# Scale and shift of the second norm: from the stored token rows to the transposed gathered tokens

## The chip, the cores and the metric

The kernel runs on one core of a Trainium2 chip. The core has five engines, each with an instruction queue of its own that runs in order: PE (TensorE, matmuls and transposes; its weight loads are listed as PEld), DVE (VectorE), ACT (ScalarE), POOL (GpSimd) and SP (SyncE, which here only issues DMAs). The engines wait for each other on semaphores. On-chip tiles lie in SBUF, matmul results in PSUM, the rest in DRAM. The metric is the device time of one execution in microseconds.

## What is computed

One layer of an encoder on 1024 tokens of 1024 channels in float32. A conditioning vector gives `shift1, scale1, gate1, shift2, scale2, gate2`. After the mixer has been added to `x`, the part that matters here is:

```python
h2 = rmsnorm(x, norm2_w) * (1.0 + scale2) + shift2          # per channel
aff = softmax(h2 @ w_router)                                # 16 experts
gates, idx = top_k(aff.transpose, 128)                      # each expert picks 128 tokens
xe = h2[idx]                                                # gather
y = (silu(xe @ w_gate) * (xe @ w_up)) @ w_down              # per expert, 1024 wide
x += gate2 * scatter_add(idx, y * gates)
```

`rmsnorm` divides a token's row by its root mean square `r` and multiplies by `norm2_w` per channel. So `h2` is `x` times a number per token, then a scale and a shift per channel.

## The kernel before

The framework in which the kernel is written takes the instructions in program order, with tiles from pools. A pool tag has a number of buffers, and a tile waits for a free one. A scheduling pass with durations of its own then fixes an order for each engine's queue. `issue_after(ins)` keeps instructions behind `ins` on the same engine.

**Projection stage** (`w_o`, L1278). Eight tiles of 128 tokens. For each tile, `wo_tile` (L1335) runs the output projection on PE; every factor is split into a high part, rounded to the matmul type, and the low rest, and three products (high-high, high-low, low-high) are summed. `wo_post` (L1352) follows for the tile before: it loads `x` (L1356, SP), adds the projection (L1359, DVE), transposes (PE, through the helper at L149), squares and sums the rows (L1368, ACT), gets `r` on DVE (`rsqrt1`, L125), computes the router's scores from the transposed rows with the scale already folded into `wr` (L1309) and the shift into `rc` (L1308), takes the softmax (L1376 to L1382; the exponential L1380 is ACT's) and transposes the scores. Then, in tiles 0 to 6, L1395 on DVE computes `x * r * g2`, where `g2` is the scale of all channels broadcast to 128 partitions; in the last tile this is L1398 on ACT and L1399 on POOL. L1400 on POOL adds the broadcast shift `sh2`, and L1401 (POOL's DMA queue) stores the row tile of `h2` to DRAM. `rsqrt1` returns -8 times the wanted factor, so the -0.125 in `g2` puts that right. `g2`, `sh2` and `norm2_w` come as broadcast DMAs on SP (L1290, L1291), and L1292 and L1293 combine them. The same vectors are also loaded as columns into `cols` (L1298 to L1303): columns 0 to 7 the shift, 8 to 15 the scale of the eight blocks of 128 channels.

Sorting the scores is DVE work too: `best_merge` after tile 3, `join_best` after tiles 5 and 7 and `threshold` at the end, made of `max`, `match_replace` and a merge network (`bitonic`, L1439 and L1440, min and max of 16x64 tiles; L1482 and L1484 on 16x128). From the threshold `choose` computes each token's slot in each expert.

**Expert stage** (`moe`, L1580), 16 experts one after the other. For expert `e`, `gather(e + 1)` is in program order first: a one-hot tile (L1543, DVE, in a buffer with the tag `y`, of which there are two), eight small matmuls (L1548), the list of rows (L1550 to L1552), and an indirect DMA on POOL's queue (L1605) that gathers 128 rows of `h2` into `xe`. The gathered rows are transposed in two halves of four blocks (`to_T`, L1592): four transposes into one PSUM tile (tag `dn`, two buffers), a cast to the high part on ACT (L1598) and a subtraction for the low part on DVE (L1599). The weights come by SP in pieces of 512 KB (24 per expert) into a ring of 31 SBUF tiles (`RING`, L39; one of its places is `hTl5`, where `sh2` lies before). Each piece is split on ACT (L1575) and DVE (L1576) into one of four pairs of tiles. PE multiplies tokens with the gate and up weights (L1629), ACT and DVE form `silu(gate) * up` (L1633, L1634, in a `y` buffer), which is transposed by `to_T` in turn, and PE multiplies with the down weights in eight blocks `k` (L1646). Within this last loop, at `k` of 5 and 6, the two halves of the next expert's tokens are transposed (L1640 to L1642). L1650 weights the result, and L1652, again on POOL's queue, adds it to the output rows in DRAM; it reads the same tile into which `xe` is gathered.

Of the kernel before, what the change touches and what calls it, by code (L numbers as in the profile page):

```python
# [7 lines left out]
F = mybir.dt.float32  # L8
# [4 lines left out]
AF = mybir.ActivationFunctionType  # L13
OP = mybir.AluOpType
# [4 lines left out]
D = 1024  # L19
S = 1024  # L20
NT = 8
C_Q, C_K, C_V, C_DQ, C_DK, C_DV, C_DZ, C_BA, C_G = 0, 512, 640, 768, 1280, 1792, 2304, 2816, 2848
EPS = 1e-6
NEXP = 16
# [61 lines left out]
class K:  # L86
# [1191 lines left out]
    def w_o(self):  # L1278
        nc, i, u, wk = self.nc, self.i, self.unit, self.ep
        self.mhl = [[u(g, (128, 8, 128), R, name="mhl") for g in gs] for gs in (("g1", "g2"), ("g14", "g15"))]  # L1280
        for ps, _ in self.wo_tile(0):
            pass
        g2, sh2 = (u(g, name="mod") for g in ("hTl4", "hTl5"))
        self.xs = [u(g, name="wx") for g in ("hTl6", "hTl7")]
        self.xTs = [u(g, (128, 8, 128), name="wxT") for g in ("hTh6", "hTh7")]
        self.ts = [u(g, name="wt") for g in ("g16", "g0", "wl")]
        self.gt2 = wk.tile([128, D], F, name="gt2")
        n2 = self.ts[2]
        for t, row in ((sh2, 1), (g2, 2), (self.gt2, 3)):
            nc.sync.dma_start(t, self.mod_d[row:row + 1].to_broadcast([128, D]))  # L1290
        nc.sync.dma_start(n2, i["norm2_w"].to_broadcast([128, D]))  # L1291
        nc.vector.scalar_tensor_tensor(g2, g2, 1.0, n2, op0=OP.add, op1=OP.mult)  # L1292
        nc.vector.tensor_scalar(g2, g2, -0.125, None, op0=OP.mult)  # L1293
        wr = wk.tile([128, 8, NEXP], F, name="wr", bufs=1)
        nc.sync.dma_start(wr, i["w_router"][0].rearrange("(k p) e -> p k e", p=128))
        rows = wk.tile([24, 128], F, name="rrows", bufs=1)
        for r, src in enumerate((self.mod_d[1:2], self.mod_d[2:3], i["norm2_w"])):
            nc.sync.dma_start(rows[r * 8:r * 8 + 8], src.rearrange("o (k p) -> (o k) p", p=128))  # L1298
        pc = self.pa.tile([128, 128], F, name="tr", bufs=2)
        self.transpose(pc[:, 0:24], rows)  # L1300
        cols = wk.tile([128, 24], F, name="rcols", bufs=1)
        nc.vector.tensor_copy(cols, pc[:, 0:24])
        nc.vector.scalar_tensor_tensor(cols[:, 8:16], cols[:, 8:16], 1.0, cols[:, 16:24], op0=OP.add, op1=OP.mult)  # L1303
        pr = self.pa.tile([128, NEXP], F, name="tr", bufs=2)
        for k in range(8):
            nc.tensor.matmul(pr, cols[:, k:k + 1].to_broadcast([128, 128]), wr[:, k], start=(k == 0), stop=(k == 7))
        rc = wk.tile([128, NEXP], F, name="rc", bufs=1)
        nc.vector.tensor_copy(rc, pr)  # L1308
        nc.vector.scalar_tensor_tensor(wr, wr, -0.125, cols[:, 8:16].unsqueeze(2).to_broadcast([128, 8, NEXP]),  # L1309
                                       op0=OP.mult, op1=OP.mult)  # L1310
        for j in range(NT):
            post = self.wo_post(j, ps, g2, sh2, wr, rc, wk)
            at = list(POSTS)
            for nxt, done in self.wo_tile(j + 1) if j + 1 < NT else ():
                while at and done > at[0]:
                    next(post, None)
                    at.pop(0)
            for _ in range(EARLY.get(j, 0)):
                self.ring_load()
            for _ in post:  # L1320
                pass
            ps = nxt
            if j == 3:
                rbest = wk.tile([NEXP, CAP], F, name="rbest", bufs=1)
                nc.scalar.copy(rbest, rev(self.best_merge(wk)))
            if j in JOINS:
                self.join_best(JOINS.index(j), rbest, wk)
        self.threshold(rbest, wk)
# [20 lines left out]
                                     start=(k == 0 and n == 0), stop=(k == 7 and n == 2))  # L1349
            yield pq, (s + 1) / len(steps)  # L1350

    def wo_post(self, j, pq, g2, sh2, wr, rc, wk):  # L1352
        nc, i = self.nc, self.i
        sl = slice(j * 128, (j + 1) * 128)
        x, t, xT = self.xs[j % 2], self.ts[j % 3], self.xTs[j % 2]
# [15 lines left out]
        r = self.rsqrt1(wk, ss, "r2")  # L1371
# [19 lines left out]
                nc.vector.tensor_copy(self.sc[p:p + NEXP, t0], pa[:NEXP, 64 * x2:64 * x2 + 64])  # L1391
        yield
        nc.gpsimd.dma_start(self.out[0, sl, :], x)
        if j < NT - 1:
            nc.vector.scalar_tensor_tensor(t, x, r, g2, op0=OP.mult, op1=OP.mult)  # L1395
        else:
            with self.tc.issue_after(ex):
                nc.scalar.activation(t, x, AF.Copy, scale=r)  # L1398
            nc.gpsimd.tensor_mul(t, t, g2)  # L1399
        nc.gpsimd.tensor_add(t, t, sh2)  # L1400
        nc.gpsimd.dma_start(self.h2_d[sl, :], t)  # L1401


# [176 lines left out]
    def moe(self):  # L1580
# [11 lines left out]
        def to_T(dst, src, q):  # L1592
# [5 lines left out]
            nc.scalar.copy(hi, pt)  # L1598
            nc.vector.tensor_sub(lo, pt, hi.bitcast(F))  # L1599

        def gather(e):
            nonlocal found
            with self.tc.issue_after(found) if e else ExitStack():
# [8 lines left out]
        gather(0)  # L1612
        first = found
        for q in range(2):
            to_T(xT, xe[:, q * 512:(q + 1) * 512], q)
        for e in range(NEXP):
            if e + 1 < NEXP:
                gather(e + 1)
# [18 lines left out]
            for k in range(8):  # L1637
                if k == 2:
                    to_T(aT, acts[1], 1)
                if e + 1 < NEXP and k in (5, 6):  # L1640
                    q = k - 5
                    to_T(xT, xe[:, q * 512:(q + 1) * 512], q)  # L1642
                w = weights()
                for n, (x, wi) in enumerate(passes(aT, w)):
                    for q in range(2):
# [41 lines left out]
```

## Time and profile before

| | us |
|---|---|
| median of 3 runs (lowest, highest) | 1728.37 (1728.33, 1729.34) |
| the profiled execution | 1728.42 |
| its span, first to last instruction | 1726.6 |
| PE, DVE, ACT, POOL busy | 1616.8, 1409.3, 907.1, 204.3 |

"Busy" is the time in which an engine had an instruction running, over the whole span. Matmuls are pipelined, and their ends are modelled, so a busy PE need not be PE at its best rate. In the lists in order of time, neighbouring instructions of one form are merged (x4 is four of them), and brackets tell how long the engine was idle before and what ended the wait.

### The profile page before, as it was taken

The numbers are of one execution on the slowest core, as the hardware profiler recorded it, in microseconds if no ns is written. First come the engines' busy times: TensorE is split into PE (matmuls) and PEld (weight loads), VectorE is DVE, ScalarE is ACT, GpSimd is POOL, SyncE is SP. The second block draws the span as 40 slices with busy tenths as digits, with TensorE's granted clock in tenths as the row PEclk, the third lists the DMA queues.
The fourth block names the chain that finished last, engine by engine and source line by source line (L and its number), as shares of the span: only waits on it lengthen the run. The fifth ranks groups of instructions, "written<-read, shape, count | busy, mean of one in ns | idle before, by whom it ended". The sixth has DMA issues, their size and how long they took to land. (4 is left out here: it accounts for less than half of the span.)

```text
span 1726.6 us, 30147 instructions
## 1 busy us (share of the span) xinstructions
PE 1616.8 (94%) x11131; PEld 1278.1 (74%) x11131; DVE 1409.3 (82%) x2470; ACT 907.1 (53%) x1352; POOL 204.3 (12%) x196
## 2 busy tenths in 40 slices
PE   6999999889999899699999999669999999999997
PEld 4777778677777677478887788557777777777786
DVE  6899897954667757789986567979999999999996
ACT  6654432122344213288871323347777777777775
POOL 0000022010100100021112312300011000110000
PEclk9999999998999999699999999879999999999999
DMA  9454377257778966721135464769999999999981
GB/s 280 129 175 131 104 181 195 82 179 171 184 197 225 273 176 182 196 86 38 38 111 182 155 209 147 259 227 351 384 379 374 382 388 383 375 377 384 385 309 25
DMA packets 284146, 388.81 MB, mean 225 GB/s; under 512 B 88219, under 2 KB 152399, under 8 KB 283487
## 3 DMA queue, kind: packets, MB, share of 16 engines
q1 hardware_dynamic: 263279, 325.54, 57.4%
q0 software_dynamic: 14096, 48.77, 10.3%
q10 hardware_dynamic: 6624, 12.59, 2.0%
q8 instruction: 88, 1.44, 0.4%
q14 instruction: 59, 0.48, 0.1%
HBM read 328.04 MB, written 58.77 MB: 224 GB/s over the span
## 5 line engine op out<-in xcount | busy, mean ns | idle before, releaser
L1576 DVE TENSOR_TENSOR ew<-er,ew 128x1024 fp32r<-128x1024 f32 x384 | 452.2, 1219 | 29.8 <-ACT ew L1575 29.7
L1575 ACT CAST ew<-er 128x1024 fp32r<-128x1024 f32 x384 | 391.0, 1049 | 137.9 <-PE pj L1629 105.4
L1629 PE MATMUL pj<-ew,xT 128*128 128x512 f32 x1536 | 367.6, 396 | 4.5 <-DVE ew L1576 4.5
L1629 PEld LDWEIGHTS pj<-ew,xT 128*128 128x128 f32 x1536 | 283.2, 188 | 76.2 <-DVE ew L1576 19.5
L1646 PE MATMUL tr<-ew,aT 128*128 128x512 f32 x768 | 191.3, 398 | 0.0
L1646 PEld LDWEIGHTS tr<-ew,aT 128*128 128x128 f32 x768 | 139.7, 188 | 30.4 <-DVE ew L1576 3.4
L297 PE MATMUL pj<-hTh,wl 128*128 128x512 f32 (+1 forms) x384 | 123.4, 399 | 6.5 <-DVE wl L279 6.5
L297 PE MATMUL pj<-hTh,wh 128*128 128x512 f32 (+1 forms) x384 | 122.0, 397 | 3.3 <-ACT hTh L258 1.8
L297 PE MATMUL pj<-hTl,wh 128*128 128x512 f32 (+1 forms) x384 | 121.5, 397 | 1.4 <-DVE hTl L261 1.4
L297 PEld LDWEIGHTS pj<-hTh,wl 128*128 128x128 f32 (+1 forms) x384 | 71.9, 188 | 23.7 <-DVE wl L279 6.9
L297 PEld LDWEIGHTS pj<-hTh,wh 128*128 128x128 f32 (+1 forms) x384 | 70.7, 187 | 20.6 <-ACT hTh L258 1.9
L866 DVE TENSOR_REDUCE am<-pj 128x1 f32<-128x1024 f32 x64 | 77.7, 1216 | 10.0 <-PE pj L861 9.5
L1652 POOL DMA_INDIRECT out_dram<-xe,idxT x16 | 37.2, 2327 | 407.9 <-DVE tok L1550 353.4
L297 PEld LDWEIGHTS pj<-hTl,wh 128*128 128x128 f32 (+1 forms) x384 | 71.2, 187 | 18.6 <-DVE hTl L261 2.0
L1255 PE MATMUL pj<-hTh,uw 128*128 128x512 f32 x256 | 83.5, 404 | 1.0 <-DVE uth L1261 0.5
L868 ACT ACTIVATE ap<-pj,am 128x1024 f32<-128x1024 f32 x64 | 71.8, 1123 | 20.7 <-DVE am L866 11.1
L1209 PE MATMUL pj<-hTh,wh 128*128 128x512 f32 x224 | 79.9, 423 | 0.8 <-ACT y L1214 0.8
L1209 PE MATMUL pj<-hTh,wl 128*128 128x512 f32 x224 | 79.4, 422 | 0.0
L1209 PE MATMUL pj<-hTl,wh 128*128 128x512 f32 x224 | 77.8, 416 | 0.0
L861 PE MATMUL pj<-kT,qT 128*128 128x512 f32 x256 | 76.3, 406 | 0.0
L278 ACT CAST wh<-wraw 128x1024 fp32r<-128x1024 f32 (+1 forms) x26 | 26.7, 1028 | 87.9 <-PE pj L297 87.9
L325 DVE SCALAR_TENSOR_TENSOR y<-xc,colt,y 128x1024 f32<-128x1024 f32 x48 | 61.4, 1279 | 1.4 <-ACT y L323 0.9
(391 smaller groups left out, 2899.0 us busy)
## 6 DMA issues: line engine op xcount, KB each, us to landing
er<-in_w_gate_dram SPq DMA_DIRECT2D x128, 512.0 KB
er<-in_w_up_dram SPq DMA_DIRECT2D x128, 512.0 KB
er<-in_w_down_dram SPq DMA_DIRECT2D x128, 512.0 KB
wraw<-in_w_in_dram POOLq DMA_DIRECT2D x36, 512.0 KB, 5.9
mw<-in_w_ada_dram SPq DMA_DIRECT2D x44, 256.0 KB
wt<-in_w_ada_dram SPq DMA_DIRECT2D x16, 512.0 KB
gate_d<-y ACTq DMA_DIRECT2D x32, 256.0 KB
kqs<-kq_d SPq DMA_DIRECT2D x32, 256.0 KB
```

What stands on the lines that cost most here:

```text
L297: self.nc.tensor.matmul(ps[q][:n], w[:, k, :n], x[k][:, q * 512:(q + 1) * 512], start=(k == 0 and w is wh and x is self.hTh), stop=(k == 7 ...
L325: nc.vector.scalar_tensor_tensor(y, xc[:, t:t + S], w(t), y, op0=OP.mult, op1=OP.add)
L861: nc.tensor.matmul(ps[:, kh], qT[:, i * 128:(i + 1) * 128], self.kT[a][:, s, kh * 512:(kh + 1) * 512], start=(s == 0), stop=(s == 1), skip ...
L866: nc.vector.reduce_max(m, ps, axis=AX.X, negate=True)
L868: nc.scalar.activation(p, ps, AF.Exp, bias=m, scale=1.0, accum_out=self.rv[:, h, half * 4 + i:half * 4 + i + 1])
L1209: nc.tensor.matmul(ps[q], a[:, k], x[k][:, q * 512:(q + 1) * 512], start=(k == 0 and a is wh and x is self.hTh), stop=(k == 7 and a is wl))
L1255: nc.tensor.matmul(ps, w[:, k], v[k][:, qs], start=(k == 0 and p == 0), stop=(k == 3 and p == 2))
L1575: nc.scalar.copy(hi, raw)
L1576: nc.vector.tensor_sub(lo, raw, hi.bitcast(F))
L1629: nc.tensor.matmul(pg[m], x[:, 2 * kp + k], wi[:, k], start=(kp == 0 and k == 0 and n == 0), stop=(kp == 3 and k == 1 and n == 2))
L1646: nc.tensor.matmul(py[q], x[:, k], wi[:, q], start=(k == 0 and n == 0), stop=(k == 7 and n == 2))
L1652: nc.gpsimd.indirect_dma_start(out=out2, out_offset=bass.IndirectOffsetOnAxis(ap=self.idx[:, e:e + 1], axis=0), in_=y, in_offset=None, com ...
```

## The change

The stored row is now only `x * r`. It is computed on ACT in all eight tiles, behind the exponential (before, in the last tile alone). The broadcast `g2`, `sh2` and `norm2_w`, their loads and L1292, L1293, L1395, L1399 and L1400 are gone; one more instruction puts -0.125 times the scale into columns 16 to 23 of `cols`. In the expert stage the tokens' transposes have a function of their own, `tokens_T`: each transposed block of 128 channels passes through an ACT activation with the block's shift and scale as per-partition columns, into an SBUF tile `h` from the two `y` buffers; the high part is cast from `h`, and the low part is `h` minus the high part. The two halves stand at `k` of 3 and 4 in place of 5 and 6.

```diff
--- before.py
+++ after.py
@@ -1280,17 +1280,11 @@
         self.mhl = [[u(g, (128, 8, 128), R, name="mhl") for g in gs] for gs in (("g1", "g2"), ("g14", "g15"))]
         for ps, _ in self.wo_tile(0):
             pass
-        g2, sh2 = (u(g, name="mod") for g in ("hTl4", "hTl5"))
         self.xs = [u(g, name="wx") for g in ("hTl6", "hTl7")]
         self.xTs = [u(g, (128, 8, 128), name="wxT") for g in ("hTh6", "hTh7")]
         self.ts = [u(g, name="wt") for g in ("g16", "g0", "wl")]
         self.gt2 = wk.tile([128, D], F, name="gt2")
-        n2 = self.ts[2]
-        for t, row in ((sh2, 1), (g2, 2), (self.gt2, 3)):
-            nc.sync.dma_start(t, self.mod_d[row:row + 1].to_broadcast([128, D]))
-        nc.sync.dma_start(n2, i["norm2_w"].to_broadcast([128, D]))
-        nc.vector.scalar_tensor_tensor(g2, g2, 1.0, n2, op0=OP.add, op1=OP.mult)
-        nc.vector.tensor_scalar(g2, g2, -0.125, None, op0=OP.mult)
+        nc.sync.dma_start(self.gt2, self.mod_d[3:4].to_broadcast([128, D]))
         wr = wk.tile([128, 8, NEXP], F, name="wr", bufs=1)
         nc.sync.dma_start(wr, i["w_router"][0].rearrange("(k p) e -> p k e", p=128))
         rows = wk.tile([24, 128], F, name="rrows", bufs=1)
@@ -1301,6 +1295,8 @@
         cols = wk.tile([128, 24], F, name="rcols", bufs=1)
         nc.vector.tensor_copy(cols, pc[:, 0:24])
         nc.vector.scalar_tensor_tensor(cols[:, 8:16], cols[:, 8:16], 1.0, cols[:, 16:24], op0=OP.add, op1=OP.mult)
+        nc.vector.tensor_scalar(cols[:, 16:24], cols[:, 8:16], -0.125, None, op0=OP.mult)
+        self.cols = cols
         pr = self.pa.tile([128, NEXP], F, name="tr", bufs=2)
         for k in range(8):
             nc.tensor.matmul(pr, cols[:, k:k + 1].to_broadcast([128, 128]), wr[:, k], start=(k == 0), stop=(k == 7))
@@ -1309,7 +1305,7 @@
         nc.vector.scalar_tensor_tensor(wr, wr, -0.125, cols[:, 8:16].unsqueeze(2).to_broadcast([128, 8, NEXP]),
                                        op0=OP.mult, op1=OP.mult)
         for j in range(NT):
-            post = self.wo_post(j, ps, g2, sh2, wr, rc, wk)
+            post = self.wo_post(j, ps, wr, rc, wk)
             at = list(POSTS)
             for nxt, done in self.wo_tile(j + 1) if j + 1 < NT else ():
                 while at and done > at[0]:
@@ -1349,7 +1345,7 @@
                                      start=(k == 0 and n == 0), stop=(k == 7 and n == 2))
             yield pq, (s + 1) / len(steps)
 
-    def wo_post(self, j, pq, g2, sh2, wr, rc, wk):
+    def wo_post(self, j, pq, wr, rc, wk):
         nc, i = self.nc, self.i
         sl = slice(j * 128, (j + 1) * 128)
         x, t, xT = self.xs[j % 2], self.ts[j % 3], self.xTs[j % 2]
@@ -1391,13 +1387,8 @@
                 nc.vector.tensor_copy(self.sc[p:p + NEXP, t0], pa[:NEXP, 64 * x2:64 * x2 + 64])
         yield
         nc.gpsimd.dma_start(self.out[0, sl, :], x)
-        if j < NT - 1:
-            nc.vector.scalar_tensor_tensor(t, x, r, g2, op0=OP.mult, op1=OP.mult)
-        else:
-            with self.tc.issue_after(ex):
-                nc.scalar.activation(t, x, AF.Copy, scale=r)
-            nc.gpsimd.tensor_mul(t, t, g2)
-        nc.gpsimd.tensor_add(t, t, sh2)
+        with self.tc.issue_after(ex):
+            nc.scalar.activation(t, x, AF.Copy, scale=r)
         nc.gpsimd.dma_start(self.h2_d[sl, :], t)
 
 
@@ -1598,6 +1589,19 @@
             nc.scalar.copy(hi, pt)
             nc.vector.tensor_sub(lo, pt, hi.bitcast(F))
 
+        def tokens_T(q):
+
+            pt = self.pa.tile([128, 4, 128], F, name="dn", bufs=2)
+            h = self.fp.tile([128, 512], F, name="y", bufs=2).rearrange("p (k c) -> p k c", k=4)
+            for k in range(4):
+                c = q * 4 + k
+                self.transpose(pt[:, k], xe[:, c * 128:(c + 1) * 128])
+                nc.scalar.activation(h[:, k], pt[:, k], AF.Identity, bias=self.cols[:, c:c + 1],
+                                     scale=self.cols[:, 16 + c:17 + c])
+            hi, lo = (t[:, q * 4:q * 4 + 4] for t in xT)
+            nc.scalar.copy(hi, h)
+            nc.vector.tensor_sub(lo, h, hi.bitcast(F))
+
         def gather(e):
             nonlocal found
             with self.tc.issue_after(found) if e else ExitStack():
@@ -1612,7 +1616,7 @@
         gather(0)
         first = found
         for q in range(2):
-            to_T(xT, xe[:, q * 512:(q + 1) * 512], q)
+            tokens_T(q)
         for e in range(NEXP):
             if e + 1 < NEXP:
                 gather(e + 1)
@@ -1637,9 +1641,9 @@
             for k in range(8):
                 if k == 2:
                     to_T(aT, acts[1], 1)
-                if e + 1 < NEXP and k in (5, 6):
-                    q = k - 5
-                    to_T(xT, xe[:, q * 512:(q + 1) * 512], q)
+                if e + 1 < NEXP and k in (3, 4):
+                    q = k - 3
+                    tokens_T(q)
                 w = weights()
                 for n, (x, wi) in enumerate(passes(aT, w)):
                     for q in range(2):
```

## Rows read from the trace of the kernel before

**Rows 1.** Busy time by stretch: stretch, length, busy us (instructions) per engine, PEclk, DMA share, GB/s.
```profile
1000.00:1072.00 72.00, 72.00 (x384) 60.48 (x382) 49.28 (x151) 21.85 (x58) 15.64 (x14) 1.00 0.46 156
...
1090.00:1108.00 18.00, 15.78 (x81) 12.64 (x80) 16.94 (x90) 7.72 (x16) 3.47 (x3) 1.00 0.74 246
1108.00:1126.00 18.00, 4.24 (x25) 3.54 (x25) 17.00 (x90) 4.67 (x13) 7.84 (x9) 0.57 0.83 309
...
1396.00:1432.00 36.00, 35.70 (x170) 28.50 (x169) 34.13 (x37) 27.18 (x30) 4.30 (x2) 1.00 1.04 384
```
**Rows 2.** Order in time, DVE, end of the projection: start, duration, instruction, [idle before].
```profile
1097.87 1.27 DVE L1395 SCALAR_TENSOR_TENSOR wt<-wx,r_y,mod 128x1024 f32<-128x1024 f32 x1
...
1099.83 1.97 DVE L1482 TENSOR_TENSOR bx<-by,sr 16x128 f32<-16x128 f32 x1 [0.42 <-ACT sr L1481]
...
1108.03 0.67 DVE L1359 TENSOR_TENSOR wx<-wx,pj 128x512 f32<-128x512 f32 x1
...
1115.02 0.21 DVE L1440 TENSOR_TENSOR by<-bx 16x64 f32<-16x64 f32 x1
...
1115.41 2.40 DVE L1440 TENSOR_TENSOR bx<-by 16x64 f32<-16x64 f32 x1
...
1118.17 2.37 DVE L1440 TENSOR_TENSOR by<-bx 16x64 f32<-16x64 f32 x1
```
**Rows 3.** Order in time, POOL, the same stretch.
```profile
1099.29 2.37 POOL L1400 TENSOR_TENSOR wt<-wt,mod 128x1024 f32<-128x1024 f32 x1 [4.94 <-DVE wt L1395]
...
1115.40 2.33 POOL L1399 TENSOR_TENSOR wt<-wt,mod 128x1024 f32<-128x1024 f32 x1
```
**Rows 4.** Order in time, PE, the same stretch.
```profile
1088.77 0.27 PE L149 MATMUL tr<-masks,aff 128*16 128x128 f32 x1 [0.80 <-DVE aff L1382]
...
1103.65 0.27 PE L149 MATMUL tr<-masks,aff 128*16 128x128 f32 x1 [1.04 <-DVE aff L1382]
...
1106.32 0.39 PE L1348 MATMUL pj<-hTl,mhl 128*128 128x512 f32 x1
```
**Rows 5.** Instructions by line and form, ACT, whole span: busy us, mean ns of one.
```profile
L1575 ACT CAST ew<-er 128x1024 fp32r<-128x1024 f32 x384 | 391.0, 1049 | 137.9 <-PE pj L1629 105.4 <-PE tr L1646 16.7 <-DMA er<-in_w_gate_dram 5.1
...
L258 ACT ACTIVATE hTh<-xT,mod,g 128x1024 fp32r<-128x1024 f32 x8 | 10.0, 1244 | 18.4 <-DVE g L250 18.4
...
L764 ACT CAST vst<-tr 128x128 fp32r<-128x128 f32 x8 | 2.2, 274 | 0.0
...
L1633 ACT ACT_TABLE_LOAD x1 | 1.3, 1283 | 0.0
```
**Rows 6.** Chain that ended last, at the first gather: start, duration, what.
```profile
1135.20 4.95 DMA xe<-h_d,idxT
...
1140.29 1.94 PE dn L149 x8
```
**Rows 7.** Order in time, all engines, one expert.
```profile
1395.21 1.40 DVE L1650 SCALAR_TENSOR_TENSOR xe<-tr,gate,gt 128x512 f32<-128x512 f32 x2
...
1397.88 3.48 DVE L1576 TENSOR_TENSOR ew<-er,ew 128x1024 fp32r<-128x1024 f32 x3
...
1399.14 13.12 PE L1629 MATMUL pj<-ew,xT 128*128 128x512 f32 x56 [0.30 <-DVE ew L1576]
...
1407.29 1.92 POOL L1605 DMA_INDIRECT xe<-h_d,idxT  x1 [8.01 <-DVE ew L1576]
...
1418.17 1.22 DVE L1543 TENSOR_TENSOR y<-cnt,slot 128x1024 bf16<-128x1024 f32 x1
...
1425.41 0.60 PE L149 MATMUL dn<-masks,xe 128*128 128x128 f32 x4
...
1431.11 1.41 DVE L1650 SCALAR_TENSOR_TENSOR xe<-tr,gate,gt 128x512 f32<-128x512 f32 x2
```
**Rows 8.** Order in time, all engines, the last expert.
```profile
1681.78 16.84 PE L1629 MATMUL pj<-ew,xT 128*128 128x512 f32 x72
...
1715.73 1.41 DVE L1650 SCALAR_TENSOR_TENSOR xe<-tr,gate,gt 128x512 f32<-128x512 f32 x2 [2.64 <-PE tr L1646]
```

## The prediction

> **What bounds the kernel now.** I read the page's busy shares first, but they mix stages, so then the busy time by stretch [rows 1], then the order in time on each engine where the change works, then one expert of the last stage. Before 1072 us the output projection is PE's: 72.00 of 72.00 us busy in 1000 to 1072, DVE 49.28. From there DVE takes over, because sorting the router's scores is one long DVE queue: 16.94 and 17.00 of 18 us in the two stretches that follow, with PE down to 15.78 and 4.24. From 1142 us on the experts run, and two engines share the limit: in a period of 36 us PE is busy 35.70, DVE 34.13, ACT only 27.18.
>
> In the DVE-bound stretch look at the lengthened instructions [rows 2]. L1440 on a 16x64 tile takes 0.21 us, yet two of them take 2.40 and 2.37, and L1482 takes 1.97. Now the POOL instructions of the same moments [rows 3]: the add L1400 runs from 1099.29 to 1101.66, and L1482 ends at 1101.80; the multiply L1399 runs from 1115.40 to 1117.73, and the first long L1440 ends at 1117.81. The second long L1440 pairs in the same way with the last L1400, 2.7 us later. A short DVE instruction with two inputs in SBUF that starts beside a 1024-column POOL add ends just behind it. So DVE pays for POOL's work.
>
> **What it removes.** (a) Seven L1395 on DVE (1.27 us each) and nine POOL instructions, eight L1400 and L1399. For tiles 0 to 4 that is worth nothing: PE is the cover, with no idle time in 1000 to 1072. From tile 5 on it counts. PE twice waits for DVE's L1382, 0.80 us at 1088.77 and 1.04 us at 1103.65 [rows 4]. Ahead of L1382 in DVE's queue stand the L1395 of the tile, 1.27 us, and one lengthened instruction, L1482 in tile 6 with some 1.7 us more than it needs (tile 5 has the same pair). Without them the waits go, and PE's last projection matmul, which starts at 1106.32 and takes 0.39, ends 1.84 us sooner. The residual add L1359 that follows it started at 1108.03, 1.32 us after PE was done, held by the same queue, which is now about 5.9 us shorter (two pairs of 1.27 and 1.7). So PE is late next, and L1359 moves by 1.84 + 1.32 = 3.2 us; I take **3.0**. Behind it the two long L1440 lose 2.40 - 0.21 and 2.37 - 0.21, **4.35** us, straight on the chain to the first gather, since DVE has 1 us idle in those 18. Lower end of this term: 4.35 alone; upper end: all DVE time freed from tile 5 on, 5.9 + 4.35 = 10.3.
>
> (b) In the setup three broadcast loads of 512 KB (g2, sh2, n2), L1292 and L1293 go, and one 8-column instruction comes; PE is full there: 0. SP's queue is only shorter by it.
>
> (c) Tile hTl5 no longer waits for POOL, so the weight load that reuses it goes out earlier, with those behind it on SP. Its data is used by expert 1: 0.
>
> **What it adds and moves.** (d) x*r on ACT for seven more tiles, at most 1.24 us each as L258 [rows 5], behind the tile's exponential. ACT is busy 7.72 of 18 us there: 0. Without this cover it would be seven times 1.24 behind PE, and only tiles 5 and 6 are near the chain: 2.5. The load of x for tile j+2 waits for the last reader of x, now this one, up to 5.8 us later than L1395 (1097.87, against 1103.65 for the scores' transpose, which the exponential precedes); that load, and the weight loads queued behind it on SP, have a tile's time or more in hand, 14.9 us between the two scores' transposes [rows 4]. The store of h2 leaves POOL's queue earlier.
>
> (e) Ahead of expert 0 the gather lands, then eight transposes take 1.94 us, 0.24 each [rows 6], and a cast follows the fourth. Now four activations of 128 columns come between. No row has this form, so I bound it: a 128-column cast takes 0.27 (L764); L258 with scale and bias as columns takes 1.24 against 1.05 for a cast as wide (L1575), so the two columns cost 0.20, together **0.47** us. Four in a row are 1.9 us against 1.0 for the transposes under them: **+0.9**, between 0.4 (only the last one shows) and 1.9 (all four).
>
> (f) In each of 15 later experts: eight such activations, 3.8 us of ACT; ACT goes from 27.2 to 31.0 of 36. DVE's two subtractions stay, with both inputs in SBUF. The gather for the next expert was issued at 1407.29, the transposes of its tokens stood at 1425.41 [rows 7], and a gather takes 4.95 from issue [rows 6]. They move from weight blocks 5 and 6 to 3 and 4, some 2.8 us sooner (12 matmuls at 16.84 / 72 [rows 8]), so the gather is covered still. The buffers named y now hold h as well, in order of allocation, so the one-hot tile of the next expert (L1543, 1.22 us, at 1418.17) can start only when h's first half is read. What does an expert lose now? The last expert, without gather work, takes 1681.78 to 1715.73, 33.95 us; with two groups of transposes of 0.60 each that is 35.2, and a period takes 35.90 (1395.21 to 1431.11). So 0.7 us is PE waiting for a DVE that is behind, as the 0.30 at 1399.14 shows. The change's cost per expert lies between -0.7 (the new order removes this lag) and +3.8 (all of ACT's addition shows). I take **0**: ACT has 8.8 us free, and DVE, the tighter of the two, gets no more work.
>
> The row of DVE splits at 1397.88, three with two SBUF inputs in 3.48 us, runs beside POOL's scatter and isn't lengthened, so I put nothing on the new subtraction. The Trainium skill (SBUF — State Buffer, Who interferes with whom) says that a DVE instruction with two SBUF inputs is blocked by a GpSimd instruction that reads SBUF; were POOL's indirect DMA such a one, the new subtraction would be exposed where the old one, with one input in PSUM, was not. The same section infers that issuing DMAs is not, and this row agrees.
>
> **Sum.** -3.0 - 4.35 + 0.9 + 0 = -6.45 us against the profiled execution's 1728.42 (its span of 1726.6 and 1.8 around it; the median of the runs, 1728.37, is the same): **1722.0 us**. Its own range, with (a), (e) or (f) (within 0.2 us per expert) at an end and the others as taken, is 1719 to 1725.
>
> **The rivals.** *ACT's queue takes over (slower).* In the down half the activations stand in one in-order queue with the casts that feed DVE; L1543 leaves its early place there too. If DVE starves by what L1543 costs, 1.2 us per expert, it is 15 x 1.2 - 6.45 = +11.5, 1739.9 us; from 0.43 us per expert on it eats the whole gain. For it: PE already waits on DVE's splits, and DVE has 1.9 us free per period. Against it: ACT's 8.8. Chance 0.25, of which 0.12 near the break-even at about 1728.
>
> *The lag goes too (faster by more).* If the earlier transposes and the later L1543 bring DVE's work into better order, 0.7 us per expert comes back: 15 x 0.7 = 10.5 more, 1711.5 us. For it: PE has nothing else to wait for. Against it: DVE's total stays. Chance 0.15.
>
> *The long DVE instructions have another cause.* Then 4.35 stays and 3.0 - 0.9 is left: 1726.3 us. Against it: the ends match POOL's within 0.15 us. Chance 0.08.
>
> *Table loads.* If Identity needs another table than Silu, two loads of 1.283 us (L1633, the only one in this stage) come per expert: 15 x 2 x 1.283 = 38.5, 1760.4 us. The casts there cause none, but no row shows Identity beside Silu. Chance 0.02. It is that low because the Trainium skill (ScalarE: Activation LUTs, Table sets: the hidden batching unit) lists identity among the cheap functions that every table set holds; no run here shows it, and by its price of about 2.66 us per switch this rival would be at 1802.
>
> **How the numbers follow.** Forecast 0.50. A measurement of this kernel can tell about 0.2%, 3.5 us, from no change. Faster: 0.48 of the forecast, 0.15, and 0.02 of the third rival, 0.65. Same: 0.02, 0.12 and 0.06, 0.20. Slower: 0.13 and 0.02, 0.15. The range, **1708 to 1733**, takes in the second and third rivals and the first up to 0.7 us per expert, and leaves out nearly 0.2.
>
> **What would show it.** Right: no POOL add after 1000 us, no 16-row DVE instruction above 0.4 us, the first gather issued near 1127.8 instead of 1135.20, a period of 35.9 +- 0.2 us, activations of 0.4 to 0.5 us. Wrong: long DVE instructions without POOL beside them; a period above 36.3, with PE waiting for DVE splits and DVE for ACT in the down half; a table load per Silu.

## The result, and the profile after

The time rose instead of falling: 1744.58 us (median of 4 runs, 1744.27 to 1748.61) against 1728.72 in the same comparison, a ratio of 1.0097 (95% interval 1.0079 to 1.0114). The forecast was 1722.0, with a range to 1733. The profiled execution's span grew from 1726.64 to 1742.67 us, by 16.0.

In the changed kernel L1534 is the one-hot tile (L1543 before), L1566 and L1567 are the casts and splits of the weights, L1599 the new activations, L1602 and L1603 the tokens' cast and subtraction, L1633 and L1650 the gate/up and down matmuls, L1654 the weighting of the result, L1609 the gather. First the busy time by stretch, the columns as in [rows 1].

```profile
1000.00:1072.00 72.00, 72.00 (x378) 60.20 (x376) 34.34 (x146) 26.03 (x63) 4.91 (x9) 1.00 0.48 159
1090.00:1108.00 18.00, 17.13 (x90) 13.77 (x88) 16.34 (x96) 10.08 (x21) 1.85 (x4) 1.00 0.86 291
1108.00:1126.00 18.00, 4.21 (x35) 3.40 (x34) 15.32 (x102) 3.36 (x10) 3.24 (x7) 0.61 0.84 322
1396.00:1432.00 36.00, 34.95 (x166) 27.34 (x164) 33.31 (x37) 28.75 (x38) 2.91 (x2) 1.00 1.02 369
```

Until 1126 us it went as intended: POOL has less to do, DVE is less full, and PE waits less. In the experts PE lost: 34.95 of 36 us busy, against 35.70.

To find where, I set common marks in both traces: the scores' constant (L1306, now L1302), the gather, the first gate matmul, and the weighting that ends each expert. The mark in the setup of the projection, first of before, then of after:

```profile
1005.08 1.85 PE L1306 MATMUL tr<-wr,rcols 128*128 128x16 f32 x16
```
```profile
1006.44 1.85 PE L1302 MATMUL tr<-wr,rcols 128*128 128x16 f32 x16
```

It comes 1.36 us later, though the changed kernel has less to do up to here (L1292 and L1293, 1.9 us of DVE, and three loads are gone). In the traces of the changed kernel and of those below it lies between 1003.1 and 1008.6; the two ends are e9 and e13, which have the same instructions in the same order on every compute engine up to the mark. So I take it for a difference between executions, not of the change, and the comparisons start from the mark.

| stretch | before | after | difference |
|---|---|---|---|
| start to the mark | 1005.08 | 1006.44 | +1.36 |
| mark to the gather's issue | 130.12 | 123.87 | -6.25 |
| gather to the first gate matmul | 6.90 | 10.44 | +3.54 |
| to the end of expert 0 | 37.64 | 38.45 | +0.81 |
| 13 periods of 35.92, now 37.01 | 466.92 | 481.10 | +14.18 |
| the last two experts | 69.07 | 71.56 | +2.49 |

With what follows the last expert's weighting (10.91 us before, 10.82 after) this is the 16.0. So the projection gave 6.25 us, and 21 went back behind the gather's issue.

The 0.81 us up to the end of expert 0 are not clearly the tokens': in e4 below, whose tokens are as before, the same stretch is 38.22 us, 0.58 more than before. The first 7.90 us of the gate matmuls, before and in e4, columns as in [rows 1] (PEclk, third from the end, is the granted share of 2.4 GHz):

```profile
1142.10:1150.00 7.90, 7.90 (x38) 6.25 (x38) 4.45 (x8) 4.00 (x5) 0.97 (x1) 0.84 0.63 219
```
```profile
1138.42:1146.32 7.90, 7.90 (x35) 6.15 (x35) 4.12 (x7) 3.44 (x4) 0.97 (x1) 0.77 0.64 214
```

PE was busy only 8.04 of the 34.10 us from 1108 to 1142.10 before, with a granted share of 0.54: TensorE's clock had fallen from 2.4 to 1.2 GHz. It is still at the lower level when expert 0 begins, and in e4 for more of these 7.90 us. As an estimate from the two shares, 0.84 and 0.77, that costs 0.55 us, about the 0.58 measured. The changed kernel has 0.67 there, 1.3 us by the same estimate; what gives 0.5 of it back was not looked into.

In front of expert 0, order in time, all engines:

```profile
1130.31 1.24 POOL L1609 DMA_INDIRECT xe<-h_d,idxT  x1 [14.21 <-DVE idxT L1542]
...
1135.83 0.66 PE L149 MATMUL dn<-masks,xe 128*128 128x128 f32 x2 [6.76 <-DMA xe<-h_d,idxT]
1136.32 0.81 ACT L1599 ACTIVATE y<-dn,rcols 128x128 f32<-128x128 f32 x2 [15.74 <-PE dn L149]
...
1136.83 0.82 PE L149 MATMUL dn<-masks,xe 128*128 128x128 f32 x2 [0.34 <-ACT y L1599]
...
1137.34 0.81 ACT L1599 ACTIVATE y<-dn,rcols 128x128 f32<-128x128 f32 x2 [0.22 <-PE dn L149]
...
1140.75 4.63 PE L1633 MATMUL pj<-ew,xT 128*128 128x512 f32 x10 [1.05 <-ACT xT L1602]
```

The transposes do not run on under the activations, as before [rows 6]; they alternate with them, about 0.51 us for each block. In the code a transpose and the activation that reads it follow each other on one PSUM tile, and from the third on each transpose waits for ACT.

Now one expert, order in time, all engines (to be held against [rows 7]):

```profile
1401.19 1.41 DVE L1654 SCALAR_TENSOR_TENSOR xe<-tr,gate,gt 128x512 f32<-128x512 f32 x2
...
1403.11 1.22 DVE L1534 TENSOR_TENSOR y<-cnt,slot 128x1024 bf16<-128x1024 f32 x1
...
1405.52 0.96 PE L1633 MATMUL pj<-ew,xT 128*128 128x512 f32 x3 [0.78 <-DVE ew L1567]
...
1406.72 13.15 PE L1633 MATMUL pj<-ew,xT 128*128 128x512 f32 x56 [0.24 <-DVE ew L1567]
...
1430.18 0.27 PE L149 MATMUL dn<-masks,xe 128*128 128x128 f32 x1
...
1434.56 0.80 ACT L1599 ACTIVATE y<-dn,rcols 128x128 f32<-128x128 f32 x2
1434.69 1.23 DVE L1567 TENSOR_TENSOR ew<-er,ew 128x1024 fp32r<-128x1024 f32 x1 [0.35 <-ACT ew L1566]
...
1436.36 1.23 DVE L1567 TENSOR_TENSOR ew<-er,ew 128x1024 fp32r<-128x1024 f32 x1 [0.44 <-ACT ew L1566]
...
1437.20 0.27 PE L149 MATMUL dn<-masks,xe 128*128 128x128 f32 x1
```

Two things differ. The one-hot tile, at 1418.17 in the middle of the old expert, now stands at 1403.11, at the head of the next one and ahead of weight splits for which PE then waits 0.78 and 0.24 us (0.30 before). And between 1430 and 1438, while the tokens are transposed one block at a time, DVE waits for ACT's weight casts, where before it ran without a gap. The waits over twelve experts say the same (us in total, times, longest). Before:

```profile
DVE ew L1576 <- ACT ew L1575: 19.6, 60, 0.4
DVE aT L1599 <- ACT aT L1598: 2.9, 12, 0.2
...
PE pj L1629 <- DVE ew L1576: 3.6, 12, 0.3
```

After:

```profile
DVE ew L1567 <- ACT ew L1566: 32.0, 96, 0.5
...
PE pj L1633 <- DVE ew L1567: 12.2, 24, 0.8
```

DVE waits 9.5 us more for ACT in twelve experts, 0.8 each, and PE 0.7 each more for DVE. That is not all of the 1.09 us: PE's busy time grew too, from 35.62 to 35.93 us per period, with the transposes given one at a time. Weight transfers are not the cause: ACT waited 6.6 us for them in twelve experts before and not at all after.

### The profile page after: what moved, and what is told of

The parts are those of the page before. It is cut to its first block, busy times and chain, and to the rows that moved or that the text cites. A ratio compares the mean times of both kernels' runs of the same rounds, so it can differ in the third digit from the quotient of the medians.

```text
span 1742.7 us, 30156 instructions
## 1 busy us (share of the span) xinstructions
PE 1624.9 (93%) x11131; PEld 1276.9 (73%) x11131; DVE 1389.9 (80%) x2462; ACT 956.6 (55%) x1487; POOL 176.6 (10%) x187
## 4 chain that ended last, share of the span: by engine, by line
PE 72%; DVE 14%; DMA 6%; issue 4%; ACT 2%; SPq 1%; POOL 0%; POOLq 0%; DVEq 0%; ACTq 0%
PE pj L1633 16%; PE pj L297 11%; PE tr L1650 9%; PE pj L1209 7%; PE pj L1344 5%; PE pj L1255 4%; PE dn L149 4%; PE tr L149 3%; PE pj L861 3%; PE tr L885 2%; DVE ew L1567 2%; PE tr L884 2%; DVE xe L1654 1%; DVE y L1534 1%; PE dn L669 1%
## 5 line engine op out<-in xcount | busy, mean ns | idle before, releaser
L1567 DVE TENSOR_TENSOR ew<-er,ew 128x1024 fp32r<-128x1024 f32 x384 | 455.0, 1221 | 42.6 <-ACT ew L1566 42.6
L1566 ACT CAST ew<-er 128x1024 fp32r<-128x1024 f32 x384 | 390.9, 1047 | 117.7 <-PE pj L1633 106.4
L1633 PE MATMUL pj<-ew,xT 128*128 128x512 f32 x1536 | 369.3, 396 | 15.8 <-DVE ew L1567 14.8
L1633 PEld LDWEIGHTS pj<-ew,xT 128*128 128x128 f32 x1536 | 285.0, 189 | 86.2 <-DVE ew L1567 27.0
L1650 PE MATMUL tr<-ew,aT 128*128 128x512 f32 x768 | 198.9, 406 | 0.0
L1650 PEld LDWEIGHTS tr<-ew,aT 128*128 128x128 f32 x768 | 139.3, 191 | 25.1
L1656 POOL DMA_INDIRECT out_dram<-xe,idxT x16 | 28.1, 1755 | 460.8 <-DVE xe L1654 460.8
```

What stands on the lines that cost most here:

```text
L1566: nc.scalar.copy(hi, raw)
L1567: nc.vector.tensor_sub(lo, raw, hi.bitcast(F))
L1633: nc.tensor.matmul(pg[m], x[:, 2 * kp + k], wi[:, k], start=(kp == 0 and k == 0 and n == 0), stop=(kp == 3 and k == 1 and n == 2))
L1650: nc.tensor.matmul(py[q], x[:, k], wi[:, q], start=(k == 0 and n == 0), stop=(k == 7 and n == 2))
```

## The experiments

Each ratio below is against runs of the kernel before on the same chip, whose medians were 1728.5 to 1730.4 us. All periods are means over 13 experts, from the weighting that ends expert 0 to that of expert 13 (after: 1179.20 to 1660.30). The first theories: **A**, the y buffer shared with `h` displaces the one-hot; **B**, the alternation of transposes and activations makes the tokens late; **C**, ACT's added work.

**e1: a buffer of its own for `h`.**

```diff
-            h = self.fp.tile([128, 512], F, name="y", bufs=2)
+            h = self.ep.tile([128, 512], F, name="h", bufs=1)
```

> The changed kernel with one edit: h has a buffer of its own and no longer takes one of the two y buffers, so the one-hot tile of the next expert need not wait for h. Theory A (the shared buffer puts the one-hot at the head of the next expert, where PE waits for the weight splits behind it): the one-hot goes back into the down half, the period falls from 37.01 to 35.9 us and the time from 1744.6 to 1728. Theory B (each transpose waits for the activation before it, so the tokens' last cast and subtraction come only after the next expert has begun): that chain is untouched, so at least the 0.57 us that the last expert loses by it stays in each period: 36.5 us, 1737. Theory C (ACT's 3.8 us more per expert): nothing changes, 37.0 us, 1744.6.

Measured: 36.37 us, 1734.67 us, ratio 1.0031 (1.0021 to 1.0041). Some 0.64 us per expert come back, which speaks for A with a rest of B's size; in its trace PE waits 6.7 us in twelve experts for the tokens' subtraction (L1603), which is B's wait. What e1 also changed I saw only later: one buffer in place of two lets ACT's second half start only when the first is read.

**e2: the transposes of a half together, then its activations.**

```diff
             for k in range(4):
                 c = q * 4 + k
                 self.transpose(pt[:, k], xe[:, c * 128:(c + 1) * 128])
+            for k in range(4):
+                c = q * 4 + k
                 nc.scalar.activation(h[:, k], pt[:, k], AF.Identity, ...
```

> The changed kernel with one edit: the four transposes of a half are issued together, then the four activations, so that no transpose waits for an activation; h still shares the y buffers. A: the one-hot still waits for h, but h is free sooner; it must still stand at the end of the down half or at the head of the next expert, so at most half of the loss comes back: 36.4 to 37.0 us per expert, 1734 to 1743. B: the loss goes, 35.9 us; in front of expert 0 the time from the gather's issue to the first matmul of the gate falls from 10.44 by some 2 us: 1726. C: 37.0 us, 1742.5.

Measured: slower still, 37.59 us, 1753.33 us, ratio 1.0139 (1.0121 to 1.0158). No theory had that. In front of expert 0 the edit did gain: 8.71 us from the gather to the first gate matmul, against 10.44 (0.35 of it because the gather took 5.17 us to the first transpose, not 5.52). So the alternation is what cost there, but in the later experts the grouping cost more than it gave.

**e3: both edits.**

> Both edits: h in a buffer of its own and the four transposes together. A and B: 35.9 us per expert or a little less, and 2 us less in front of expert 0: 1724 to 1726, faster than the kernel before. C: 37.0 us, 1742.5.

Measured: 35.92 us, exactly the period of before, and 1725.96 us, ratio 0.9978 (0.9968 to 0.9989): faster than before, with all eight activations in each expert. C in its plain form (3.8 us more work on ACT) falls. Order in time, all engines; L1601 and L1604 are the activations and the tokens' cast here:

```profile
1397.05 13.14 PE L1635 MATMUL pj<-ew,xT 128*128 128x512 f32 x56 [0.29 <-DVE ew L1567]
...
1416.11 1.22 DVE L1534 TENSOR_TENSOR y<-cnt,slot 128x1024 bf16<-128x1024 f32 x1
...
1421.05 4.62 DVE L1567 TENSOR_TENSOR ew<-er,ew 128x1024 fp32r<-128x1024 f32 x4
1421.69 1.50 ACT L1601 ACTIVATE h<-dn,rcols 128x128 f32<-128x128 f32 x4
...
1423.07 1.06 ACT L1566 CAST ew<-er 128x1024 fp32r<-128x1024 f32 x1
1424.01 0.64 ACT L1604 CAST xT<-h 128x512 fp32r<-128x512 f32 x1
1424.53 2.25 ACT L1566 CAST ew<-er 128x1024 fp32r<-128x1024 f32 x2
...
1426.68 1.50 ACT L1601 ACTIVATE h<-dn,rcols 128x128 f32<-128x128 f32 x4
```

When ACT turns to the tokens (1421.69), DVE is at the first of four splits without a gap and two more pieces are as good as cast; the fourth is cast between ACT's two halves.

**e4: the projection part alone.** Scale and shift are left out of the tokens, whose transposes are as before, at blocks 5 and 6.

```diff
-                    tokens_T(q)
+                    to_T(xT, xe[:, q * 512:(q + 1) * 512], q)
```

> The projection stage as changed, the tokens' transposes and their place as before: scale and shift of the second norm are left out of the tokens altogether. The gather's place tells what the projection stage gives by itself. If the forecast's terms (a) hold: 7.35 us, 1721.0. As the changed kernel's trace has it, 4.9 us against the trace before, of which 1.4 more are taken by a stage whose instructions are the same: 1722.2 to 1723.5. If the long DVE instructions had another cause than POOL: 1726. The period stays at 35.9 us.

Measured: 1723.76 us, ratio 0.9959 (0.9945 to 0.9973); 123.85 us from the mark to the gather, 6.27 less than before; 35.91 us per expert; 6.79 from the gather to the first gate matmul.

**e5: POOL's add put back into e4** (the scale is left out).

```diff
+        nc.gpsimd.tensor_add(t, t, self.sh2)
         nc.gpsimd.dma_start(self.h2_d[sl, :], t)
```

> As e4 (the projection stage as changed, the tokens as before, the scale left out), with one thing put back: POOL adds the broadcast shift to each row tile behind ACT's multiplication. If POOL's 1024-column add holds back DVE instructions with two SBUF inputs: 16-row DVE instructions of 2 to 2.4 us are back beside each add after tile 4 (0.5 us at most in e4), two to three of them, and the first gather comes 2 to 6 us later than e4's 1131.63. If the long instructions had another cause: none above 0.6 us, gather within 1.5 us of e4's.

Measured (one run, 1728.88 us): 129.62 us from the mark (1005.51) to the gather, 5.77 more than e4. Order in time, POOL:

```profile
1105.22 2.41 POOL L1394 TENSOR_TENSOR wt<-wt,mod 128x1024 f32<-128x1024 f32 x1 [9.43 <-ACT wt L1393]
...
1117.49 2.34 POOL L1394 TENSOR_TENSOR wt<-wt,mod 128x1024 f32<-128x1024 f32 x1
...
1135.13 1.25 POOL L1612 DMA_INDIRECT xe<-h_d,idxT  x1 [13.84 <-DVE idxT L1545]
```

and DVE:

```profile
1105.39 2.32 DVE L1433 TENSOR_TENSOR by<-bx 16x64 f32<-16x64 f32 x1
...
1117.51 2.40 DVE L1434 TENSOR_TENSOR bx<-by 16x64 f32<-16x64 f32 x1
```

The long instructions are back, each beside an add and done within 0.1 us of its end, without L1395 on DVE. That is what the Trainium skill (SBUF — State Buffer, Who interferes with whom) says of a DVE instruction with two SBUF inputs beside a GpSimd instruction that reads SBUF; here an instruction of 0.21 us takes 2.3 to 2.4.

So POOL's adds alone can cost 5.77 us. How the 6.25 us of the change divide between POOL's hold and the 1.27 us of each L1395 is not shown, for here the adds come later, behind ACT's multiplication, and cost at other places: 2.00 us up to the transpose of tile 5's scores (L149), 2.14 from there to the second residual add and 1.63 behind it. The change gained 0.96, 1.80 and 3.49 in these three stretches. The last of them is that of the two long L1440 and has no L1395.

**e6: one copy in place of the four activations** (scale and shift are left out), otherwise e2.

```diff
-                nc.scalar.activation(h[:, k], pt[:, k], AF.Identity, ...
+            nc.scalar.copy(h, pt)
```

> The changed kernel with the four transposes together and one 512-column copy on ACT in place of the four activations (scale and shift of the second norm are left out); h still shares the y buffers. ACT's addition is then 1.2 us per expert in place of 3.8, and no transpose waits for ACT. Theory A, sharpened by e1 and e2 (what counts is that the one-hot and the tokens' last subtraction stand in DVE's unbroken run at the end of the expert, where each us shows at the head of the next): still 0.7 to 1.8 us above 35.9. Theory C (ACT's load): 35.9 to 36.2.

Measured: 36.05 us, 1726.09 us, ratio 0.9983 (0.9973 to 0.9994). My sharpened A missed: the one-hot is late here too, behind both subtractions of the tokens, and costs 0.13 us. What is gone is ACT's long stretch.

**e7: the halves back at blocks 5 and 6**, otherwise as changed.

> The changed kernel with the transposes of the tokens back at the blocks 5 and 6. If the earlier place did the harm: 35.9 us per expert. If the shared buffer and the alternation of transposes and activations do it: the one-hot and the tokens come later still, 37.0 to 38.2 us per expert, 1744 to 1763.

Measured: 38.21 us and 1761.97 us (one run). The earlier place was no harm but a help of 1.2 us per expert, of which 0.4 is a lower clock (see below the table).

**e9 and e10: e2's order on ACT with the one-hot early.** e9 puts the one-hot ahead of the tokens in program order, e10 gives `h` two buffers of its own.

```diff
+                if k == 2 and e + 2 < NEXP:
+                    hot(e + 2)
                 if e + 1 < NEXP and k in (3, 4):
```

> e2 with one edit: the next one-hot tile, its small matmuls and the list of rows stand in program order ahead of the tokens (at block 2 of the down half), so the one-hot takes a y buffer before h does; h still shares the two y buffers, and ACT's queue has the same order as in e2 (five activations in a row, a cast of the tokens, three more). If the displaced one-hot is the cause of e2's 37.7 us: 35.9 to 36.1 us per expert, 1726. If it is ACT's unbroken run of activations, with the weight casts behind it and DVE waiting for both: 36.5 to 37.7 us, 1734 to 1752.

> e3 with a second buffer for h (taken from the ring of weight pieces, 30 places in place of 31). ACT's queue then has e2's order (five activations, a cast, three activations) while the one-hot stands early as in e3. Displaced one-hot: 35.9 us per expert, 1726. ACT's run of activations: 36.5 us or more, 1734 or more; the single buffer of e3 would then have helped by keeping weight casts between the two halves.

Measured: 37.75 us and 37.50 us; ratios 1.0129 (1.0113 to 1.0144) and 1.0124 (1.0107 to 1.0141). With the one-hot early and even with no shared buffer, e2's loss stays: it is ACT's unbroken run. (e10 has one place less in the ring, but in its trace ACT never waits for a weight transfer in the experts after the first.) In e10, order in time, all engines:

```profile
1403.19 15.86 PE L1635 MATMUL pj<-ew,xT 128*128 128x512 f32 x68 [1.54 <-DVE ew L1567]
...
1429.91 3.48 DVE L1567 TENSOR_TENSOR ew<-er,ew 128x1024 fp32r<-128x1024 f32 x3
1430.56 1.84 ACT L1601 ACTIVATE h<-dn,rcols 128x128 f32<-128x128 f32 x5
...
1432.28 0.64 ACT L1604 CAST xT<-h 128x512 fp32r<-128x512 f32 x1
1432.79 1.18 ACT L1601 ACTIVATE h<-dn,rcols 128x128 f32<-128x128 f32 x3
...
1433.83 1.08 ACT L1566 CAST ew<-er 128x1024 fp32r<-128x1024 f32 x1
...
1434.94 1.22 DVE L1567 TENSOR_TENSOR ew<-er,ew 128x1024 fp32r<-128x1024 f32 x1 [0.94 <-ACT ew L1566]
```

From 1430.56 to 1433.83 ACT casts no weights. DVE uses up its three casts, stands still for 0.94 us, and PE pays 1.55 at the head of the next expert (1440.47), as it paid 1.54 at the head of this one. In e3 DVE had as many pieces ready when ACT began; the cast between the halves is the difference that the traces show.

**e12 and e13: the two causes apart.** e12 is e2 with the halves at blocks 3 and 6: ACT's order is then e3's, the one-hot late. e13 is the changed kernel with the one-hot early as in e9.

> e2 with one edit: the two halves of the tokens stand at the blocks 3 and 6 in place of 3 and 4. h still shares the y buffers and the one-hot still waits for h; ACT's queue now has e3's order (four activations, weight cast, tokens' cast, two weight casts, four activations, weight cast, tokens' cast). If the activations in one run are the cause: 35.9 to 36.2 us per expert and 1726 to 1730. If the shared buffer and the late one-hot are: 36.5 us or more, 1735 or more.

> The changed kernel with the one-hot early as in e9 and nothing else: transposes and activations alternate as changed, h shares the y buffers. The period of the changed kernel, 37.01 us, is 1.10 above that of before. If the late one-hot is 0.66 of it, as e1 (36.35) seems to say: 36.35 us, 1735. If e1 gained by its single buffer alone and ACT's order is all: 37.0 us, 1744.

Measured: e12 36.74 us, ratio 1.0062 (1.0040 to 1.0084); e13 36.18 us, ratio 1.0031 (1.0017 to 1.0044). In e12 the late one-hot costs 0.82 us against e3 with the same order on ACT, as the second expectation had it. In e13 moving the one-hot alone returns 0.83 of the changed kernel's 1.09, more than I had taken from e1. In e13, order in time, all engines (L1637 is the gate matmul):

```profile
1402.55 13.13 PE L1637 MATMUL pj<-ew,xT 128*128 128x512 f32 x56 [0.17 <-DVE ew L1567]
...
1421.60 1.22 DVE L1534 TENSOR_TENSOR y<-cnt,slot 128x1024 bf16<-128x1024 f32 x1
...
1427.87 5.87 DVE L1567 TENSOR_TENSOR ew<-er,ew 128x1024 fp32r<-128x1024 f32 x5
```

The periods by the two causes:

| ACT's order with the tokens | one-hot early | one-hot late |
|---|---|---|
| no activations, tokens cast only | 35.92 (before) | |
| one copy and cast per half | | 36.05 (e6) |
| four activations, weight casts, four | 35.92 (e3) | 36.74 (e12) |
| one or two between weight casts | 36.18 (e13) | 37.01 (after) |
| five in a row, then three | 37.75, 37.50 (e9, e10) | 37.59 (e2) |

Not in the table are e1 (36.37, one-hot early, but its single buffer makes the tokens late) and e7 (38.21, other blocks).

Four of these means hold a lower clock too. In e2, e7, e9 and e10 the granted clock of TensorE falls from 2.4 to 1.2 GHz for a stretch in 3, 3, 1 and 2 of the 13 periods, each time during a wait of PE of 1.3 to 1.6 us near the head of an expert or within 2.2 us behind it, and these periods are 1.5 to 1.6 us longer. Two periods of e2, columns as in [rows 1]:

```profile
1176.65:1215.48 38.83, 37.25 (x169) 29.63 (x168) 34.51 (x38) 29.63 (x39) 3.98 (x2) 0.96 1.00 349
1215.48:1252.70 37.22, 35.65 (x169) 28.48 (x168) 34.40 (x38) 29.52 (x39) 3.64 (x2) 1.00 1.01 354
```

The median periods, which leave this out, are 37.24 (e2), 37.84 (e7), 37.63 (e9) and 37.27 (e10). In the other kernels the clock stays at the higher level through all 13 periods. So ACT's unbroken run itself costs 1.3 to 1.7 us per expert, and the reading of the table stays.

Both causes count, and they are not simply added. An early one-hot occupies DVE while ACT casts ahead, so DVE has splits to do during ACT's work on the tokens (the 5.87 us without a gap in e13, where one more cast piece waits for DVE at ACT's first activation than in the changed kernel). A late one takes that supply away and then stands in front of the next expert. Where ACT's run is so long that the supply ends anyway, the one-hot's place no longer matters; where ACT's work is short, it matters little. The 0.26 us that e13 keeps against before is neither of the two: PE is idle 0.22 us per period there (0.30 before) but busy 35.96 (35.62 before, 35.59 and 35.65 in e3 and e12, whose transposes are grouped). It is the alternation, as PE's own time and not as late tokens: in the changed kernel the weight loads of the tokens' transposes wait for L1599 42 times in twelve experts, 9.9 us in all.

**e8 and e11: what can be had.** e8 is e3 with the weighting, the scatter and the next one-hot and gather behind the first two weight blocks of the following expert. e11 adds scale and shift on DVE for the first half in front of expert 0.

```diff
-            if e + 1 < NEXP:
-                gather(e + 1)
...
+                    if q == 0 and kp == 2:
+                        if last:
+                            finish(*last)
+                        if e + 1 < NEXP:
+                            gather(e + 1)
```

> e3 with one more edit: the weighting of an expert's result (two DVE instructions, 1.40 us), its scatter and the next one-hot and gather stand in program order behind the first two weight blocks of the following expert, not ahead of them. If PE's loss at the head of an expert is what DVE still has to do there: the period falls from 35.92 by up to the lag of 0.65 us, to 35.3 to 35.6, and the time to 1716 to 1721. If the lag has another cause (ACT, transfers, PE's own order): 35.9 us, 1726, or longer where the gather comes too late.

> e8 with one more edit: ahead of expert 0, where DVE is idle, the scale and shift of the first half are DVE's instead of ACT's, so that the two halves go in parallel. From the gather's issue to the first matmul of the gate it was 8.73 us in e8 and 6.79 in e4 without scale and shift: 7.5 to 8.2 us are expected, 0.5 to 1.2 less than e8, 1721; the period stays at e8's 35.52 us. If DVE's instruction with two columns is slower than ACT's 0.37 us: no gain, 1722.

Measured: e8 35.51 us, 1722.06 us, ratio 0.9954 (0.9940 to 0.9967); e11 35.53 us, 1720.85 us, ratio 0.9944 (0.9931 to 0.9958). In e8, order in time, all engines (L1620 is the weighting, L1646 the gate matmul):

```profile
1425.43 3.79 PE L1646 MATMUL pj<-ew,xT 128*128 128x512 f32 x16
1425.64 0.74 DVE L1620 SCALAR_TENSOR_TENSOR xe<-tr,gate,gt 128x512 f32<-128x512 f32 x1
...
1429.21 0.75 DVE L1620 SCALAR_TENSOR_TENSOR xe<-tr,gate,gt 128x512 f32<-128x512 f32 x1
1429.35 5.92 PE L1646 MATMUL pj<-ew,xT 128*128 128x512 f32 x23
```

PE no longer waits at the head, and 0.4 us of the lag is gone. The front of e11 gained nothing clear: 8.65 us against 8.73. Its halves do not run in parallel as expected: `h` is a single buffer, and ACT's first activation waits until DVE's subtraction has read it (1138.58, behind the first gate matmul at 1137.80). The two versions beat both kernels; between e8 and e11 the intervals do not decide.

## Why the prediction was wrong

**(a), the projection: right, 1.1 us too large.** Forecast 7.35, measured 6.25, and the same within 0.05 us in every other trace without POOL's add. From the mark to the second residual add it was 2.7 us less (forecast 3.0), from there to the gather 3.5 (forecast 4.35). PE's waits for L1382 are gone, and no 16-row instruction takes 2 us. But two that take 0.21 otherwise take 0.50 now, order in time, DVE:

```profile
1114.64 0.50 DVE L1430 TENSOR_TENSOR by<-bx 16x64 f32<-16x64 f32 x1
1115.07 0.51 DVE L1431 TENSOR_TENSOR by<-bx 16x64 f32<-16x64 f32 x1
```

They account for 0.6 of the 0.85 missing there. They lie beside POOL's small instructions of the choice; the second ends 0.09 us behind POOL's 128x128 subtraction L1500 (1115.01 to 1115.49), and which one holds the first was not tried. (b), (c) and (d), costed at nothing, show nothing: PE has no idle time in 1000 to 1072, and behind it ACT is busy 10.08 of 18 us (7.72 before [rows 1]).

**(e), in front of expert 0: wrong, +3.54 for +0.9.** Of the 3.54, 0.43 lies ahead of the first transpose (5.52 us from the gather's issue, 5.09 before) and 3.11 behind it. The price of an activation was right (0.45 alone, 0.47 forecast). The step that failed is "four in a row are 1.9 us against 1.0 for the transposes under them": in the code as changed nothing runs under them, and the first cast (1140.09) comes behind all eight blocks, not behind four as before. e3, where the transposes run on, has +1.64, inside the bounds of 0.4 to 1.9.

**(f), the later experts: wrong, +1.09 us each for 0.** The step that failed is "ACT has 8.8 us free, and DVE, the tighter of the two, gets no more work". Both halves of it are true of the whole period, and e3 shows that the work fits. But ACT's free time lies mostly in the gate and up half, where it waits for PE. Before, ACT is busy 16.05 of 22.80 us there (1395.21 to 1418.01), but 11.18 of 13.12 in the down half: 1.9 us are free for 3.8 us of activations, and they fall where DVE lives on what ACT has just cast. The prediction saw that the one-hot would move and still took the mean of the period against it. The one-hot's place is 0.83 of the loss (e13), the alternation of transposes and activations the other 0.26, the latter as busy time of PE and not as a wait for splits. The range's lower bound of -0.7 and upper one of +3.8 held; the value chosen between them did not. For the clock at the start of expert 0 the prediction had no term.

**The rivals.** "ACT's queue takes over" is what happened, with its place and its two parts: DVE waits for ACT, and L1543 has left its early place. That its price came out so near, 1.2 us per expert forecast and 1.09 measured, is in part luck: the one-hot is 0.83 of it, and the rest is the alternation, which the rival did not have. Its 1739.9 also lacked the 2.6 us of (e). It was given 0.25, and the range was cut at 0.7 us per expert inside it. The reason against it, ACT's 8.8 us, was again a mean. "The lag goes too" did not happen by this change; e8 shows that some of it can be had. "Another cause" of the long instructions falls with e5. Table loads: one in this stage as before (L1637), none beside the activations. That agrees with what the Trainium skill (ScalarE: Activation LUTs, Table sets: the hidden batching unit) says of identity. The new subtraction with two SBUF inputs takes 0.69 us (688 ns in the mean of 32) as the old one with one in PSUM did (685), also where it runs beside POOL's scatter, so the indirect DMA does not hold DVE here.

The signs named for "wrong" were the right ones: a period above 36.3, PE waiting for splits and DVE for ACT in the down half.

## What to carry to other kernels

Where two engines feed each other, free time of an engine counts only in the stretch in which the new work falls: ask how much finished input its consumer has in hand there, and for how many microseconds the new work stops the supply. A tile that borrows a shared buffer can move an instruction that has nothing to do with the change; find who asks for that buffer next, and what stands behind it in its queue. If a change is right but costs at one place, try its parts apart before giving it up: here the order of the same instructions made the difference between 1.4% slower and 0.2% faster, and with one more move 0.5%.

## What I had not expected of the hardware

Activations of 128 columns on ACT take 0.45 us alone and 0.37 each in a run of five (1.84 us), so putting them together saves ACT's time, and yet it was the slowest order for the kernel at these blocks. And the same instructions in the same order reached the mark at 1003.1 to 1008.6 us in different executions: without a common mark, that is nearly as large as the gain that was to be measured. The granted clock can fall inside the experts too: in e2 a period with such a fall took 38.83 us, the next one 37.22.
